# Key and value projections between the state products, the linear unit's result kept in SBUF, and the output stage's rows in the state operands' place

## The chip, the core and the metric

The kernel runs on one core of one Trainium2 chip. The metric is the device time of one execution in microseconds (us). The core has a matrix engine (TensorE, PE in the profile, with its weight loads shown apart as PEld), a vector engine (VectorE, DVE), an engine for activations (ScalarE, ACT), a general one (GpSimd, POOL) and a fifth that only issues transfers (SyncE, SP). Each engine works through its own instructions in order; semaphores tie them together. Transfers (DMAs) are issued here from SP and, for a few, from POOL. Tiles live in SBUF, results of matmuls in PSUM.

## The reference

One layer of an encoder over 1024 tokens of width 1024. After an input LayerNorm, one projection `h @ w_in` makes the operands of three mixers: retention (256 columns), a bidirectional linear state-space mixer, S5 (256), and windowed attention (512; 8 query heads, 2 key/value heads, a window of 128 tokens to each side). The mixers' results are concatenated, go through `w_out`, and a residual LayerNorm follows; a router then lets each of 16 experts take 128 tokens, the experts are SwiGLU networks (1024 to 2048 to 1024), and a last LayerNorm follows. What the change touches:

```python
# end of the S5 mixer
y = jax.nn.gelu(y + d * uf)                       # y: sum over both scan directions
gate = jax.nn.sigmoid(y @ w_glu + b_glu)          # gated linear unit
y_ssm = y * gate
# attention
scores = jnp.einsum('bcqkgd,bcskd->bckgqs', qb, kb) - slopes * jnp.abs(rel)
p = jnp.exp(scores - m)
# output projection
mix = jnp.concatenate([y_ret, y_ssm, y_att], axis=-1) @ w_out
```

## The kernel before

All matmuls that need float32 accuracy on large operands are done as three matmuls of rounded parts: each operand is split into a high part (ACT copies it to the rounded type) and a low part (DVE subtracts), helper `split`, lines 70 and 71, and `mm3`, lines 79 to 81.

The program has four stages.

1. The **front** (`front`, from L944; 0 to about 303 us). Input norm, all projections, retention, the S5 scan and the S5 output. Its order is written out by hand: every step is put at a place, a number, and `Plan.run` emits all steps sorted by place. So each engine's queue holds the instructions in the order of places, and an instruction that waits holds up everything behind it on its engine.
2. The **attention and output loop** (from L2233; about 303 to 480 us): eight tiles of 128 tokens, two rounds for each. `attention_scores` and `attention_exp` run two rounds ahead; `attention_out` normalizes, transposes and multiplies with the values; `out_proj_load` fetches a tile's operands; `out_proj_part` projects. This loop is not ordered by hand: a planner with its own costs orders it.
3. The last tile and the choice of tokens (`last_tile`), ordered by hand.
4. The experts (about 520 us to the end): 384 weight blocks of 1 MB, each loaded, split and multiplied.

The end of the front is what the change rewrites. Its steps there, in the order list of L1162 (letters as in the code): `q31` is the last query projection, `V0` and `V1` are the value projections of the two halves of the tokens, `K0` and `K1` the key projections (24 matmuls of 128x512 each), and `o0` to `o3` the four state products (`Output.product`, 16 pairs of weight load and matmul each, with the Gelu in `Output.put`, L819). The order before is `q31 V0 o0 K0 o1 V1 o2 K1 o3`.

- A state product needs a tile `MU` (m_d and u_d), a tile `W` (wo_d) and a tile `Z` (s_d), loaded from DRAM by SP. The operands of o0 and o1 (`MU`, `W`) and the `Z` of o0 lie in pool `s5m`. The rest lies in pool `s5o`, opened by `output_space` at place O, which comes after R; R is where `keys_space` closes the retention pools `retB` and `ret`, 15 places after r7, the last retention chunk. `s5o` gets memory that `retB` leaves, so its first writers wait for the last users of `retB`, among them the store of the last retention chunk (`Chunk.store`, L436, tile `roT`).
- `key_rows` (L857) splits the keys into partitions 0 to 63 of `KHL` and copies them to partitions 64 to 127, the high part on ACT (L864), the low part on DVE (L865).
- After o3 come the gated linear unit and the first two rounds of attention scores. `Output.turn` transposes the Gelu's result (L827) and ACT copies it (L828). `Output.gate` multiplies with `w_glu` in full float32 (L833). `Output.gated` does a Tanh on ACT (L841), a scale and shift on DVE (L842) and a product on DVE (L843), into `YO`. `YO` is stored to DRAM (L847), and `out_proj_load` reads it back tile by tile (L1376), together with the retention rows (L1374), and splits both in one pair of instructions of 512 columns.
- The splits of `w_out` (`Matrix.parts`, tile `WO`) lie among these steps; so do the two rounds of `attention_exp` (L1334 and L1336), both after all the gates.

Of the kernel before, what the change touches and what calls it, by code (L numbers as in the profile page):

```python
# [20 lines left out]
P = 128  # L21
# [326 lines left out]
class Chunk:  # L348
# [84 lines left out]
    def store(self):  # L433
        oT = self.K.retB.tile([P, 2, P], F32, name="roT", bufs=2)
        self.K.nc.scalar.activation(oT, self.pt[:, 0:2, :], AF.Copy)
        self.K.nc.sync.dma_start(self.K.y_dram[self.t], oT)  # L436
# [333 lines left out]
class Output:  # L770


    def __init__(self, K, I):
        self.K, self.I, self.x = K, I, {}

    def space(self, pool):
        K, I, self.pool = self.K, self.I, pool
        self.YG = pool.tile([P, 8, 256], F32, name="YG", tag="yg")
        self.wg = pool.tile([P, 2, 256], F32, name="wg")
        K.nc.sync.dma_start(self.wg, I["ssm_w_glu"])  # L780
        self.bg = pool.tile([P, 2], F32, name="bg")
        K.nc.sync.dma_start(self.bg, I["ssm_b_glu"])

    def bias(self):
        self.hb = self.pool.tile([P, 2], F32, name="hb")
        self.K.nc.vector.tensor_scalar(self.hb, self.bg, 0.5, None, op0=OP.mult)

    def load(self, g2, q, pool, bufs):
# [6 lines left out]
        w = pool.tile([P, 2, 4, 144], F32, name="W", bufs=bufs)  # L795
# [26 lines left out]
    def turn(self, m, q):  # L822
        if m == 0 and q == 0:
            self.yT = self.pool.tile([P, 2, 8, P], F32, name="yT")
# [3 lines left out]
        self.K.nc.scalar.activation(self.yT[:, m, q * 4:q * 4 + 4, :], pt, AF.Copy)  # L828

    def gate(self, m, q):  # L830
        self.pg = self.K.pmm.tile([P, 4, P], F32, name="mm")
        for c in range(2):
            self.K.nc.tensor.matmul(self.pg, self.wg[:, c, m * P:(m + 1) * P], self.yT[:, c, q * 4:q * 4 + 4, :],  # L833
                                    start=(c == 0), stop=(c == 1))

    def gated(self, m, q):
        K, nc = self.K, self.K.nc
        if m == 0 and q == 0:
            self.YO = self.pool.tile([P, 2, P, 8], F32, name="YO", tag="yg")
        g = self.pool.tile([P, 4, P], F32, name="glu", bufs=2)  # L840
        nc.scalar.activation(g, self.pg, AF.Tanh, bias=self.hb[:, m:m + 1], scale=0.5)  # L841
        nc.vector.tensor_scalar(g, g, 0.5, 0.5, op0=OP.mult, op1=OP.add)  # L842
        nc.vector.tensor_tensor(self.YO[:, m].rearrange("p k i -> p i k")[:, q * 4:q * 4 + 4, :], g,  # L843
                                self.yT[:, m, q * 4:q * 4 + 4, :], OP.mult)
# [12 lines left out]
def key_rows(K, p, half):  # L857
# [28 lines left out]
def attention_query(K, parts, u, half):  # L886
# [3 lines left out]
                                     op1=OP.subtract)  # L890
    qs = qs.rearrange("p s (a b) -> p s a b", a=4)
# [7 lines left out]
class Matrix:  # L899
# [10 lines left out]
    def parts(self, c):  # L910
# [4 lines left out]
        for i in range(2):  # L915
            hi, lo = (K.WO[s][c // 4][:, c % 4 + i, :] for s in range(2))
            split(K, hi, lo, self.raw[c][:, i, :])
# [26 lines left out]
def front(K, I, pool, close):  # L944
# [180 lines left out]
    qs = [(g2, q) for g2 in range(2) for q in range(2)]  # L1125
# [17 lines left out]
    at(e2 + 7.0, lambda: out.states(*qs[0], X["s5m"][1]))  # L1143
# [18 lines left out]
    order = "q00 g0 g1 q01 r0 q10 r1 g2 r2 g3 q11 r3 q20 g4 r4 g5 q21 r5 g6 r6 q30 g7 r7 q31 V0 o0 K0 o1 V1 o2 K1 o3".split()  # L1162
# [3 lines left out]
    for w in order:  # L1166
        where[w] = s
        if w[0] in "KVq":
# [20 lines left out]
        elif w[0] == "r":  # L1189
# [1168 lines left out]
```

## Time and profile before

| what | value |
|---|---|
| median of 3 runs | 1634.75 us (1632.62 to 1634.87) |
| the profiled execution, its own time | 1636.51 us |
| its span, first to last instruction | 1634.6 us |
| mean granted TensorE clock | 0.987 |
| PE busy | 1568.8 us (96%) |
| DVE busy | 1418.9 us (87%) |
| ACT busy | 1130.8 us (69%) |

| stretch of the span | PE busy | granted clock |
|---|---|---|
| 0 to 231 us (front up to r7) | 216.63 of 231 us | 0.99 |
| 231 to 303 us (end of the front) | 57.31 of 72 us | 0.92 |
| 303 to 480 us (loop) | 166.90 of 177 us | 0.98 |
| 480 to 520 us (last tile) | 34.67 of 40 us | 1.00 |
| 520 to 1634 us (experts) | 1093.29 of 1114 us | 0.99 |

The timeline lists instructions by their start in us from the start of the span, then their duration, engine, line, operation and tiles; square brackets give the idle time of the engine before it and what ended that. A row of the view by stretches gives the length, then the busy time of PE, PEld, DVE, ACT and POOL with the number of instructions, the granted clock of TensorE, the busy share of the DMA engines and GB/s.

### The profile page before, as it was taken

The numbers are of one execution on the slowest core, as the hardware profiler recorded it, in microseconds if no ns is written. First come the engines' busy times: TensorE is split into PE (matmuls) and PEld (weight loads), VectorE is DVE, ScalarE is ACT, GpSimd is POOL, SyncE is SP. The second block draws the span as 40 slices with busy tenths as digits, with TensorE's granted clock in tenths as the row PEclk, the third lists the DMA queues.
The fourth block names the chain that finished last, engine by engine and source line by source line (L and its number), as shares of the span: only waits on it lengthen the run. The fifth ranks groups of instructions, "written<-read, shape, count | busy, mean of one in ns | idle before, by whom it ended". The sixth has DMA issues, their size and how long they took to land.

```text
span 1634.6 us, 21145 instructions
## 1 busy us (share of the span) xinstructions
PE 1568.8 (96%) x7704; PEld 1290.4 (79%) x7704; DVE 1418.9 (87%) x1742; ACT 1130.8 (69%) x1276; POOL 210.1 (13%) x247
## 2 busy tenths in 40 slices
PE   6999998799998999999999999999999999999997
PEld 5887887587776788888888888888878788888885
DVE  7986863777789999898998989889989999999996
ACT  4645454875755677777777777777778788787873
POOL 4002110011011010101101011001213022120211
PEclk9999999899999999999999999999999999999998
DMA  5565476424227899999999999999999999999993
GB/s 179 202 162 138 117 226 195 141 78 149 65 91 293 313 369 386 399 401 386 378 384 381 384 377 377 379 412 411 405 403 404 405 410 414 417 414 408 410 412 151
DMA packets 103258, 507.83 MB, mean 311 GB/s; under 512 B 13041, under 2 KB 28145, under 8 KB 52466
## 3 DMA queue, kind: packets, MB, share of 16 engines
q1 hardware_dynamic: 87426, 476.60, 75.0%
q0 software_dynamic: 15728, 29.89, 6.3%
q8 instruction: 60, 0.98, 0.2%
q14 instruction: 44, 0.36, 0.1%
HBM read 462.40 MB, written 44.04 MB: 310 GB/s over the span
## 4 chain that ended last, share of the span: by engine, by line
PE 49%; DVE 22%; DMA 14%; issue 8%; ACT 5%; POOL 1%; SPq 0%; POOLq 0%; DVEq 0%; ACTq 0%
PE gu L1822 19%; DVE whl L1869 11%; PE y L1822 9%; DMA wraw<-in_exp_w_down 8%; PE mm L79 4%; PE mm L81 4%; PE mm L80 4%; DMA wraw<-in_exp_w_up 4%; ACT whl L1862 2%; DMA wraw<-in_exp_w_gate 2%; DVE hT L71 1%; PE po L1362 1%; PE tp L1807 1%; DVE hid L1904 1%; DVE pT L71 1%
## 5 line engine op out<-in xcount | busy, mean ns | idle before, releaser
L1869 DVE TENSOR_TENSOR whl<-wraw,whl 128x2048 fp32r<-128x2048 f32 x384 | 870.9, 2286 | 70.2 <-ACT whl L1862 68.1
L1862 ACT ACTIVATE whl<-wraw 128x2048 fp32r<-128x2048 f32 x384 | 735.8, 1919 | 248.3 <-PE gu L1822 62.4
L1822 PE MATMUL gu<-whl,xT 128*128 128x512 f32 x3072 | 732.2, 395 | 0.0
L1822 PEld LDWEIGHTS gu<-whl,xT 128*128 128x128 f32 x3072 | 571.0, 189 | 117.4
L1822 PE MATMUL y<-whl,hT 128*128 128x512 f32 x1536 | 359.1, 389 | 0.7 <-ACT hT L70 0.7
L1822 PEld LDWEIGHTS y<-whl,hT 128*128 128x128 f32 x1536 | 288.1, 188 | 60.7 <-ACT hT L70 0.9
L1786 POOL DMA_INDIRECT xs<-h_d,index x15 | 30.0, 1999 | 461.0 <-PE y L1822 301.4
L79 PE MATMUL mm<-hT,whl 128*128 128x512 f32 x160 | 65.7, 411 | 0.0
L70 ACT ACTIVATE hT<-tp 128x512 fp32r<-128x512 f32 x80 | 46.0, 583 | 26.8 <-PE tp L1807 13.7
L81 PE MATMUL mm<-hT,whl 128*128 128x512 f32 x160 | 62.5, 391 | 0.0
L80 PE MATMUL mm<-hT,whl 128*128 128x512 f32 x160 | 62.5, 391 | 0.0
L71 DVE TENSOR_TENSOR hT<-tp,hT 128x512 fp32r<-128x512 f32 x80 | 54.0, 682 | 5.4 <-ACT hT L70 5.3
L79 PE MATMUL mm<-WO,yh 128*128 128x512 f32 x128 | 51.6, 403 | 3.6 <-ACT yh L70 3.6
L80 PE MATMUL mm<-WO,yh 128*128 128x512 f32 x128 | 50.3, 393 | 0.0
L81 PE MATMUL mm<-WO,yl 128*128 128x512 f32 x128 | 48.9, 392 | 0.0
L1807 PE MATMUL tp<-ident,hid 128*128 128x128 f32 x256 | 39.3, 276 | 9.8 <-DVE hid L1904 9.7
L1807 PEld LDWEIGHTS tp<-ident,hid 128*128 128x128 f32 x256 | 31.3, 141 | 20.1 <-DVE hid L1904 13.1
L79 PE MATMUL mm<-whl,hT 128*128 128x512 f32 (+1 forms) x128 | 46.6, 364 | 0.1
L1336 ACT ACTIVATE S<-S,asm 128x384 f32<-128x384 f32 (+1 forms) x64 | 36.9, 579 | 13.0 <-DVE asm L1323 7.7
L81 PE MATMUL mm<-whl,hT 128*128 128x512 f32 (+1 forms) x128 | 44.0, 344 | 1.4 <-DVE hT L71 1.4
L1904 DVE TENSOR_TENSOR hid<-hid,gu 128x512 f32<-128x512 f32 x64 | 43.5, 680 | 1.5 <-PE gu L1822 1.4
L80 PE MATMUL mm<-whl,hT 128*128 128x512 f32 (+1 forms) x128 | 43.9, 343 | 0.8 <-DVE whl L135 0.8
(428 smaller groups left out, 1799.3 us busy)
## 6 DMA issues: line engine op xcount, KB each, us to landing
wraw<-in_exp_w_gate SPq DMA_DIRECT2D x128, 1024.0 KB, 8.1
wraw<-in_exp_w_up SPq DMA_DIRECT2D x128, 1024.0 KB, 8.5
wraw<-in_exp_w_down SPq DMA_DIRECT2D x128, 1024.0 KB, 8.8
wraw<-in_w_in SPq DMA_DIRECT2D x8, 1024.0 KB, 7.5
x<-in_x SPq DMA_DIRECT2D x8, 512.0 KB, 4.6
h_d<-x SPq DMA_DIRECT2D x8, 512.0 KB, 3.2
q_d<-kst SPq DMA_DIRECT2D x32, 128.0 KB, 2.7
wraw<-in_w_out SPq DMA_DIRECT2D x4, 1024.0 KB, 6.8
```

What stands on the lines that cost most here:

```text
L70: nc.scalar.activation(hi, src, AF.Copy)
L71: eng.tensor_tensor(lo, src, hi.bitcast(F32), OP.subtract)
L79: nc.tensor.matmul(ps, a[0], b[0], start=start, stop=False)
L80: nc.tensor.matmul(ps, a[0], b[1], start=False, stop=False)
L81: nc.tensor.matmul(ps, a[1], b[0], start=False, stop=stop)
L1336: nc.scalar.activation(S[g][:, :W], S[g][:, :W], AF.Exp, bias=nm[:, g:g + 1], accum_out=rs[:, g:g + 1])
L1786: K.nc.gpsimd.indirect_dma_start(out=xs, out_offset=None, in_=K.h1_dram, in_offset=bass.IndirectOffsetOnAxis(ap=K.index[:, e:e + 1], axis=0))
L1807: K.nc.tensor.transpose(pt[:, c, :], src[:, (c0 + c) * P:(c0 + c + 1) * P], K.ident)
L1822: nc.tensor.matmul(ps, a[s][c], u[:, t, i * w:(i + 1) * w], start=first and id(ps) not in began, stop=last and left[id(ps)] == 0)
L1862: self.K.nc.scalar.activation(u[:, 0, :], self.raw[k1].rearrange("p a b -> p (a b)"), AF.Copy)
L1869: self.K.nc.vector.tensor_tensor(u[:, 1, :], raw, u[:, 0, :].bitcast(F32), OP.subtract)
L1904: at(self.after, q, 3, lambda: nc.vector.tensor_tensor(self.h[q], self.h[q], self.pg[q][1], OP.mult))
```

## The change

- The order becomes `q31 V0 o0 K0 V1 K1`, and the other three state products follow K1 in a section with places of its own (A): o1, o2, o3 with the scores of round 0 and the transposes between them. The products are numbered anew, so that the first two give the columns of the first transposes.
- The last retention chunk is finished earlier (`norm`, `gated`, `turn`, `store` 2.2 to 4.5 places after its product; before 4 to 12), inside q31. Its store uses a tile of another pool. R moves to just before V0, so `s5o` opens there, on the other side of the memory, and all its loads are issued from there on, `MU` and `W` now as one tile `MUW`. The store of q31's query rows goes behind them.
- The second copy of the keys is made by a DMA that POOL issues, in place of L864 and L865.
- The linear unit: the transposed values are scaled by 0.5 as they are copied, half of these copies on DVE. The Tanh takes its input unscaled, and one DVE instruction, `(tanh + 1) * y`, takes the place of two. `YO` gets a pool of its own and stays in SBUF; its two stores and the loop's sixteen loads of it are gone; the loop splits retention rows and `YO` in two pairs of 256 columns.
- `w_out` is split block by block; the first four blocks during V1, the rest in section A. The scores and exponentials of rounds 0 and 1 are issued in halves, the exponentials between the Tanhs.
- A pool `opy` opens in the place of `s5m` after o3: it holds the retention rows of two tiles, loaded in advance, and `yh` and `yl`. The loads of ln1's gain and shift come after the loop's first `out_proj_load`.

```diff
@@ Chunk.store
-        oT = self.K.retB.tile([P, 2, P], F32, name="roT", bufs=2)
+        if self.t == NT - 1:
+            oT = self.K.ast.tile([P, 2, P], F32, name="roT", tag="q2", bufs=3)
+        else:
+            oT = self.K.retB.tile([P, 2, P], F32, name="roT", bufs=2)
@@ Output
+    def weights(self):
+        K, I = self.K, self.I
         K.nc.sync.dma_start(self.wg, I["ssm_w_glu"])
         K.nc.sync.dma_start(self.bg, I["ssm_b_glu"])
...
-        x = pool.tile([P, 8, P], F32, name="MU", bufs=bufs)
+        xw = pool.tile([P, 2176], F32, name="MUW", tag="muw", bufs=bufs)
+        x = xw[:, 0:1024].rearrange("p (a b) -> p a b", a=8)
...
-        self.K.nc.scalar.activation(self.yT[:, m, q * 4:q * 4 + 4, :], pt, AF.Copy)
+        dst = self.yT[:, m, q * 4:q * 4 + 4, :]
+        if eng:
+            self.K.nc.vector.tensor_scalar(dst, pt, 0.5, None, op0=OP.mult)
+        else:
+            self.K.nc.scalar.activation(dst, pt, AF.Copy, scale=0.5)
...
-        g = self.pool.tile([P, 4, P], F32, name="glu", bufs=2)
-        nc.scalar.activation(g, self.pg, AF.Tanh, bias=self.hb[:, m:m + 1], scale=0.5)
-        nc.vector.tensor_scalar(g, g, 0.5, 0.5, op0=OP.mult, op1=OP.add)
-        nc.vector.tensor_tensor(self.YO[:, m].rearrange("p k i -> p i k")[:, q * 4:q * 4 + 4, :], g,
-                                self.yT[:, m, q * 4:q * 4 + 4, :], OP.mult)
-
-    def store(self, m):
-        self.K.nc.sync.dma_start(self.K.y2_dram[m], self.YO[:, m].rearrange("p k i -> p (k i)"))
+        g = K.ast.tile([P, 4, P], F32, name="glu", tag="k4", bufs=3)
+        nc.scalar.activation(g, self.pg.pop((m, q)), AF.Tanh, bias=self.hb[:, m:m + 1], scale=1.0)
+        nc.vector.scalar_tensor_tensor(K.YO[:, m].rearrange("p k i -> p i k")[:, q * 4:q * 4 + 4, :], g, 1.0,
+                                       self.yT[:, m, q * 4:q * 4 + 4, :], op0=OP.add, op1=OP.mult)
@@ key_rows
-        nc.scalar.activation(K.KHL[kv][b, 0, hs], K.KHL[kv][a, 0, hs].bitcast(F32), AF.Copy)
-        nc.vector.tensor_copy(K.KHL[kv][b, 1, hs], K.KHL[kv][a, 1, hs].bitcast(F32))
+        nc.gpsimd.dma_start(K.KHL[kv][b, :, hs], K.KHL[kv][a, :, hs])
@@ front
-    qs = [(g2, q) for g2 in range(2) for q in range(2)]
+    qs = [(g2, q) for q in range(2) for g2 in range(2)]
...
-    order = "q00 ... q31 V0 o0 K0 o1 V1 o2 K1 o3".split()
+    order = "q00 g0 g1 q01 r0 q10 r1 g2 r2 g3 q11 r3 q20 g4 r4 g5 q21 r5 g6 r6 q30 g7 r7 q31 V0 o0 K0 V1 K1".split()
...
-            at(s + 4, c.norm)
-            at(s + 6, c.gated)
-            at(s + 9, c.turn)
-            at(s + (12 if c.t == NT - 1 else 14), c.store)
+            for gap, fn in zip((2.2, 3.0, 3.78, 4.5) if c.t == NT - 1 else (4, 6, 9, 14),
+                               (c.norm, c.gated, c.turn, c.store)):
+                at(s + gap, fn)
...
-    R = where["r7"] + 2.9 + 12.1
+    R = where["V0"] - 0.1
...
+    at(O + 0.01, lambda: out.states(*qs[1], X["s5o"][1], 2))
+    at(O + 0.02, lambda: out.load(*qs[2], X["s5o"][1], 1))
+    at(O + 0.03, out.weights)
+    at(where["o0"] + 3.1, lambda: (out.states(*qs[2], X["s5m"][1], 1), out.load(*qs[3], X["s5m"][1], 2)))
+    at(where["o0"] + 3.2, lambda: out.states(*qs[3], X["s5o"][1], 2))
+    at(where["K0"] + 1.0, out.bias)
...
+    for (g, e1), k in zip(((0.0, 2.75), (3.2, 5.0), (6.8, 9.55)), qs[1:]):
+        at(A + g, lambda k=k: out.product(*k))
+        at(A + e1, lambda k=k: out.put(*k))
+    for g, k in ((5.9, (0, 0)), (6.0, (0, 1)), (10.3, (1, 0)), (10.35, (1, 1))):
+        at(A + g, lambda k=k: out.turn(*k, k[1]))
+    for c, hi, lo in ((4, 2.8, 2.8), (5, 2.9, 2.9), (6, 6.9, 6.9), (7, 7.0, 12.9)):
+        at(A + hi, lambda c=c: mat.high(c))
+        at(A + lo + 0.01, lambda c=c: mat.low(c))
+    for g, i, g0 in ((2.7, 0, 0), (9.5, 0, 2), (11.4, 1, 0), (13.5, 1, 2)):
+        at(A + g, lambda i=i, g0=g0: attention_scores(K, i, g0, g0 + 2))
+    for g, e1, k in ((11.8, 13.6, (0, 0)), (14.0, 15.6, (1, 0)), (15.7, 17.3, (0, 1)), (17.4, 19.0, (1, 1))):
+        at(A + g, lambda k=k: out.gate(*k))
+        at(A + e1, lambda k=k: out.gated(*k))
+    for g, i, g0 in ((10.4, 0, 0), (13.7, 0, 2), (15.65, 1, 0), (17.35, 1, 2)):
+        at(A + g, lambda i=i, g0=g0: attention_exp(K, i, g0, g0 + 2))
+
+    def rows_space():
+        close(X["s5m"][0])
+        X["opy"] = pool("opy")
+        K.opy, K.y = X["opy"][1], {}
+        for t in range(2):
+            out_proj_rows(K, t)
+    at(A + 9.6, rows_space)
@@ out_proj_load
-    y = pool.tile([P, 4, P], F32, name="y")
-    nc.sync.dma_start(y[:, 0:2, :], K.y_dram[t])
-    for m in range(2):
-        nc.sync.dma_start(y[:, 2 + m, :], K.y2_dram[m][:, t * P:(t + 1) * P])
...
-    split(K, yh[:, 0:4, :], yl[:, 0:4, :], y)
+    split(K, yh[:, 0:2, :], yl[:, 0:2, :], y)
+    split(K, yh[:, 2:4, :], yl[:, 2:4, :], K.YO[:, :, t * 16:(t + 1) * 16, :].rearrange("p m k i -> p m (k i)"))
...
+    if t + 2 < NT:
+        out_proj_rows(K, t + 2)
```

More of the change, by code (lines that the diff above doesn't have):

```diff
@@ L914, in parts, with low, part @@
                 K.WO[s].append(K.hy.tile([P, KC // 2, D], F32R, name=f"WO{s}", tag="hy"))
-        for i in range(2):
-            hi, lo = (K.WO[s][c // 4][:, c % 4 + i, :] for s in range(2))
-            split(K, hi, lo, self.raw[c][:, i, :])
+        K.nc.scalar.activation(K.WO[0][c // 4][:, c % 4, :], self.raw[c - c % 2][:, c % 2, :], AF.Copy)
+    def low(self, c):
+        K = self.K
+        hi, lo = (K.WO[s][c // 4][:, c % 4, :] for s in range(2))
+        K.nc.vector.tensor_tensor(lo, self.raw[c - c % 2][:, c % 2, :], hi.bitcast(F32), OP.subtract)
+    def part(self, c):
+        self.high(c)
+        self.low(c)
 class Rows:
@@ L1228, in keys_space @@
         K.AV = X["kv"][1].tile([P, NT, 2, 2, 64], F32R, name="AV")
+        X["yo"] = pool("yo", side="right")
+        K.YO = X["yo"][1].tile([P, 2, P, 8], F32, name="YO")
     at(R, keys_space)
@@ L1234, in output_space @@
     def output_space():
-        X["s5o"] = pool("s5o")
+        X["s5o"] = pool("s5o", side="right")
         out.space(X["s5o"][1])
-        out.bias()
     at(O, output_space)
-    at(O + 0.01, lambda: out.load(*qs[2], X["s5o"][1], 1))
-    at(O + 0.02, lambda: out.states(*qs[1], X["s5o"][1]))
-    at(where["o0"] + 3.1, lambda: (out.states(*qs[2], X["s5m"][1]), out.load(*qs[3], X["s5m"][1], 2)))
-    at(where["o1"] + 3.1, lambda: out.states(*qs[3], X["s5o"][1]))
-    G = s + 0.3
-    mq = [(m, q) for q in range(2) for m in range(2)]
-    for q in range(2):
-        at(where["K1"] + 1.9 + q * 1.9 - 0.01, lambda q=q: out.turn(0, q))
-        at(G + q * 0.5, lambda q=q: out.turn(1, q))
-    for i, k in enumerate(mq):
-        at(G + 1.7 + i * 2.0, lambda k=k: out.gate(*k))
-        at(G + 3.7 + i * 2.0, lambda k=k: out.gated(*k))
-    at(G + 11.0, lambda: (out.store(0), out.store(1)))
-    at(G + 15.0, lambda: close(X["s5o"][0], X["s5m"][0]))
+    at(O + 0.01, lambda: out.states(*qs[1], X["s5o"][1], 2))
[4 more added lines that the diff above has]
+    at(where["K0"] + 1.0, out.bias)
     mat = Matrix(K, I)
@@ L1257, in front @@
     at(where["q31"] + 8.2, lambda: mat.load(2))
-    at(where["o1"] + 0.3, lambda: (mat.parts(0), mat.load(4)))
-    at(where["K1"] + 3.0, lambda: (mat.parts(2), mat.load(6)))
-    at(G + 1.2, lambda: mat.parts(4))
-    at(G + 5.0, lambda: mat.parts(6))
+    for i, c in enumerate((0, 1)):
+        at(where["V1"] + 1.7 + i, lambda c=c: mat.part(c))
+    at(where["V1"] + 2.8, lambda: mat.load(4))
+    for i, c in enumerate((2, 3)):
+        at(where["V1"] + 3.7 + i, lambda c=c: mat.part(c))
+    at(where["V1"] + 4.8, lambda: mat.load(6))
@@ L1307, in attention_scores @@
     W, ro, k0 = (b1 - b0) * P, (b0 - c + 1) * P, b0 * P
-    qs = K.Q.pop(i)
-    sm = K.small.tile([P, 5, 4], F32, name="asm", bufs=3)
+    if g0 == 0:
+        K.P[i] = [], K.small.tile([P, 5, 4], F32, name="asm", bufs=3)
+    S, sm = K.P[i]
+    qs = K.Q[i]
     m, nm, rs, es, rd = (sm[:, k] for k in range(5))
     hs = slice(kv * 4, kv * 4 + 4)
-    S = []
-    for g in range(4):
+    for g in range(g0, g1):
         h = kv * 4 + g
@@ L2176, in build @@
     K.y_dram = [dr.tile([P, 2, P], F32, name=f"y_d{t}") for t in range(NT)]
-    K.y2_dram = [dr.tile([P, L], F32, name=f"y2_d{m}") for m in range(2)]
     K.q_dram = [[dr.tile([P, 4, 4, P], F32, name=f"q_d{h}_{k}") for k in range(2)] for h in range(2)]
```

84 lines of the change are left out of this document (45 added, 39 removed).

## The prediction

> **What bounds the kernel now.** I read the granted clock first (0.987 in the mean), then the busy time by stretches, then PE's timeline where PE is least busy, then ACT, DVE and SP at the same place. PE is busy for 96% of the span, so what the change can win is PE's idle time at the end of the front, and whatever slows PE there.
>
> ```profile
> span 1634.6 us, 21145 instructions
> PE 1568.8 (96%) x7704; PEld 1290.4 (79%) x7704; DVE 1418.9 (87%) x1742; ACT 1130.8 (69%) x1276; POOL 210.1 (13%) x247
> ```
>
> By stretches (length, then busy time of PE, PEld, DVE, ACT, POOL, then clock, DMA share, GB/s):
>
> ```profile
> 253.02:302.83 49.81, 35.12 (x181) 28.09 (x180) 26.43 (x55) 26.10 (x50) 3.65 (x10) 0.88 0.51 163
> 259.15:263.87 4.72, 4.72 (x22) 4.72 (x23) 1.75 (x2) 0.31 (x1) 0.00 (x0) 0.50 1.06 407
> 269.51:272.19 2.68, 2.68 (x26) 2.68 (x24) 0.00 (x0) 0.60 (x1) 0.00 (x0) 1.00 0.00 0
> 302.83:310.60 7.77, 7.74 (x32) 6.50 (x33) 5.10 (x18) 7.77 (x22) 0.77 (x1) 0.64 0.98 349
> 320.00:480.00 160.00, 150.43 (x807) 123.81 (x805) 125.37 (x329) 103.57 (x253) 17.18 (x45) 0.99 0.29 92
> 400.00:420.00 20.00, 16.73 (x87) 13.65 (x86) 13.61 (x42) 11.05 (x27) 2.69 (x7) 0.91 0.41 120
> ```
>
> The first row runs from the start of o1 to the loop's first transposes. Of its 49.81 us PE idles 49.81 - 35.12 = 14.69. The second row is o1 after its wait, the third is o2, the same work: 2.68 us at clock 1.00. PE's timeline says where the idle time lies:
>
> ```profile
> 231.28 0.49 PE L79 MATMUL mm<-hT,whl 128*128 128x512 f32 x1
> 236.63 0.39 PE L81 MATMUL mm<-hT,whl 128*128 128x512 f32 x1
> 253.02 0.49 PE L812 MATMUL mm<-MU 128*128 128x128 f32 x2
> 259.15 1.23 PE L815 MATMUL mm<-W,Z 128*128 128x128 f32 x4 [5.64 <-DMA Z<-s_d]
> 283.26 0.39 PE L1316 MATMUL at<-KHL,qs 128*128 128x256 f32 x1 [0.90 <-DVE asm L1320]
> 284.01 1.03 PE L827 MATMUL tp<-ident,YG 128*128 128x128 f32 x8
> 285.87 0.39 PE L1316 MATMUL at<-KHL,qs 128*128 128x256 f32 x1 [0.35 <-DVE asm L1320]
> 286.61 3.60 PE L833 MATMUL mm<-yT,wg 128*128 128x512 f32 x8
> 289.64 0.74 PE L1316 MATMUL at<-KHL,qs 128*128 128x384 f32 x1
> 290.74 3.60 PE L833 MATMUL mm<-yT,wg 128*128 128x512 f32 x8
> 302.83 1.97 PE L1355 MATMUL tp<-ident,S 128*128 128x128 f32 x8 [7.80 <-ACT S L1349]
> ```
>
> Two waits carry it. Product o1 waits 5.64 us for its `Z`. The loop's first transposes wait 7.80 us for ACT, which at the end of the gated linear unit runs behind DVE, then loads a table, then does both rounds of exponentials in one row:
>
> ```profile
> 251.08 1.28 ACT L819 ACT_TABLE_LOAD   x1 [2.79 <-DMA y_d<-roT]
> 282.36 0.60 ACT L819 ACTIVATE YG<-mm 128x512 f32<-128x512 f32 x1
> 288.53 0.69 ACT L841 ACTIVATE glu<-mm,hb 128x512 f32<-128x512 f32 x1 [0.91 <-PE mm L833]
> 296.16 0.69 ACT L841 ACTIVATE glu<-mm,hb 128x512 f32<-128x512 f32 x1 [2.81 <-DVE YO L843]
> 296.86 1.28 ACT L1334 ACT_TABLE_LOAD   x1
> 298.15 0.20 ACT L1334 ACTIVATE asm<-asm 128x4 f32<-128x4 f32 x1
> 302.29 3.29 ACT L1349 ACTIVATE S<-S,asm 128x256 f32<-128x256 f32 x8
> ```
>
> The late `Z` goes back to SP: the store of the last retention chunk holds the memory of `s5o`. From the chain of waits, SP's timeline and the view of transfers (KB each, median us to landing):
>
> ```profile
> 239.34 1.15 SPq L436 DMA_DIRECT2D y_d<-roT  x2
> 241.66 2.53 SPq L895 DMA_DIRECT2D q_d<-kst  x4
> 245.47 5.52 DMA y_d<-roT
> 251.07 0.33 SPq L780 DMA_DIRECT2D wg<-in_ssm_w_glu  x1
> 253.82 1.86 SPq L804 DMA_DIRECT2D Z<-s_d  x4
> wraw<-in_w_out SPq DMA_DIRECT2D x4, 1024.0 KB, 6.8
> Z<-s_d SPq DMA_DIRECT2D x8, 256.0 KB, 5.1
> qs<-q_d POOLq DMA_DIRECT2D x8, 256.0 KB, 3.3
> ```
>
> **The change part by part.** All sums go against the profiled execution's own 1636.51 us, whose span is 1634.6; the median of the runs is 1634.75, or 1.76 less, and I carry the difference over.
>
> *The wait for `Z` goes.* In the new order SP issues, right behind the last retention store, two `Z`, four for `MUW`, `wg`, `bg`, the `w_out` block, four query stores, and then eight more for o2 and o3: 21 issues at 0.47 (1.86 / 4) to 0.63 us (2.53 / 4), some 10.6 us. The first may have to wait for the store of chunk 6, the second of the two at 239.34 (begun about 239.9, so landed by 245.4 at the 5.52 us of its successor). So the queue is through at about 256, and the last `Z` lands 5.1 us later, at 261. PE reaches o1 only after K0, V1 and K1. Counting from the present end of K0 (253.02) these are 48 matmuls at 0.23 us ((236.63 - 231.28) / 23) and one group of transposes, about 11.6 us: 264.6 at the earliest. So all of `Z`, `MUW` and `wg` is there: -5.64 us. Behind it, DVE's `bias` waits for `bg` (issued about 249, landed about 252) ahead of the split of K0, which isn't ready before 253: nothing.
>
> *The slow clock goes with it.* After the wait the row shows clock 0.50, and o1 took 4.72 + 0.49 us where o2 takes 2.68: -2.53 us. In the new order no wait that long is left.
>
> *The other three waits.* The two short ones (0.90, 0.35) are scores that wait for DVE with two PSUM tiles; in halves, with a product or a gate between, the two pieces have 0.9 us and more in between: -1.25. The long one takes a race of PE and ACT from the end of o3 on. PE then has the scores (three halves of about 0.75, by the spacing 283.26 to 284.01), two groups of transposes (half of 0.87 each, as the next instruction shows at 284.80), four gates (half of 289.64 - 286.61 = 1.51 each), and the four heads of round 2, which the planner puts there now already (289.64 to 290.74 and the like at 293.77: 2.2): 2.25 + 0.87 + 6.06 + 2.2 = 11.4 us. ACT has the last Gelu (0.60), transposes to wait for (0.45), a copy (0.60), the table (1.28), the eight exponentials with their sums (302.29 - 298.15 = 4.14), four Tanhs (about 0.6 each when back to back: 2.4) and the first normalization (0.4): 9.9 us, and some gaps. So PE is the later one, by a little: of 7.80 us I take all but 0.5. If the planner leaves round 2 behind, PE waits up to 1 us there and does that work later.
>
> *What comes in.* Chunk 7's transposes now lie ahead of the last third of q31. Its chain isn't shortened: the gated values end at 235.52 + 0.42, while PE gets there at 231.28 + 18 x 0.23 = 235.4: +0.6. `turn` after o3 waits for the Gelu (0.60) behind scores of 0.75: +0.1. The Tanh's scale on DVE (four of 0.43) and the copies of the keys (L864, L865) fall away beside PE's work: 0. The copies become DMAs from POOL, bounded by the query loads of equal size (issue 0.75, landing 3.3 us): K0's are ready near 260 and first read near 268; K1's serve only chunk 2 and later, tens of us on: 0 at either bound.
>
> ```profile
> 235.52 0.42 DVE L425 TENSOR_TENSOR ro<-ro,gate 128x256 f32<-128x256 f32 x1 [1.42 <-ACT ro L421]
> 294.52 0.43 DVE L842 TENSOR_SCALAR glu<-glu 128x512 f32<-128x512 f32 x1
> L435 ACT ACTIVATE roT<-tp x8: 378/386/399, 182.6 to 245.1; 128x256 f32<-128x256 f32 x8
> L71 DVE TENSOR_TENSOR yl<-y,yh 128x512 fp32r<-128x512 f32 x8 | 5.5, 684 | 0.1
> L70 ACT ACTIVATE yh<-y 128x512 fp32r<-128x512 f32 x8 | 5.0, 626 | 2.7 <-PE mm L80 2.0 <-ACT asm L1334 0.7
> ```
>
> *The loop.* After 302.83 PE ran at clock 0.64 for 7.77 us, at most 2.8 us lost; but ACT is busy for all of these 7.77 us, so a faster PE waits for ACT. Between 0 and -2.8 I take -0.4, near ACT's row. Two splits of 256 columns in place of one of 512 cost ACT 2 x 0.386 - 0.626 = 0.15 and DVE 2 x 0.42 - 0.684 = 0.16 us a tile, 2.4 us for eight at most; PE is busy 150.43 of 160 us there, so I take +0.4. The stores and 16 loads of `YO` that fall away ended nobody's wait on PE in this stretch: 0. Everything behind the loop, the first weight loads too, is issued relative to the loop's rounds and moves along whole.
>
> Sum: -5.64 - 2.53 - 1.25 - 7.3 + 0.7 - 0.4 + 0.4 = -16.0 us; 1636.5 - 16.0 = 1620.5 for the profiled execution, and 1618.7 by the median.
>
> **The rivals.**
>
> *A, the loop gives a part back.* The planner orders the loop anew from another starting point. For it: stretches differ now; 400 to 420 loses 3.27 us of PE, the other seven of the loop (160 - 150.43 - 3.27) / 7 = 0.9 each. Against it: the loop's work is nearly the same. Two more stretches like that cost 2 x 2.4: -11.3, 1623.4.
>
> *B, the loads aren't early.* If SP is held until 251 as now, the state operands still arrive in time (251 + 10.6 + 5.1 = 267 for the last, needed at 272), but the second `w_out` block is issued near 255.5 and lands 6.8 later, at 262.3. ACT's split of it stands ahead of V1's copy, whose transposes PE wants at 261.3; ACT needs about 2.6 us for split and copy: +3.6, 1622.3. For it: the row at 251.07; against it: chunk 7's store no longer uses that memory.
>
> *C, tables.* The new order runs exp, Tanh, exp, Tanh and so on. One load at 251.08 served Gelu and all Tanhs; exp needed the one at 296.86. If exp and Tanh share no table, there are eight loads in place of one before the first normalization's end and a ninth behind it: +8 x 1.28 = 10.2 us on ACT, of which 1.5 are absorbed by PE's longer path: +8.7, 1627.4. No row decides it. The Trainium skill, ScalarE: Activation LUTs, section "Table sets: the hidden batching unit", lists tanh in the set of exp, and by that the extra loads don't come; the same page ("What ACT_TABLE_LOAD costs") puts a switch at about 2.66 us with its drain, by which eight would cost 21 us and the kernel would be slower. The rows here show no such drain: the load at 296.86 begins as the Tanh ends (296.16 + 0.69) and the next ACTIVATE starts at 298.15.
>
> *D, slower.* The loop becomes bound by the chain ACT, DVE, PE throughout: the doubled splits and the shifted start make every stretch of it like 400 to 420. Then it loses 8 x 3.27 = 26.2 us where it loses 9.57 now, +16.6, and the doubled splits are on the path, +2.0 more than I took: -16.0 + 18.6 = +2.6, 1637.3. It decides from 2.0 us of added PE idle time in each 20 us of the loop on. For it: such a stretch exists. Against it: the other seven.
>
> **How the numbers follow.** The forecast, 76%, own range 1615.5 to 1622 (lower with the full 2.8 us of clock, upper with B's or the splits' upper bound); A 8%, B 4%, C 4%, D 5%, and 3% for a loop that the planner orders better, some 5 us beyond the forecast. 1611.5 to 1626.5 leaves out C, D and the tails. About 0.2% of the time, 3.3 us, is what a measurement can tell from no change. Faster: all but D and a part of A that goes near it, 0.93; the same 0.02; slower 0.05.
>
> **What would show it.** Right: o1 starts with no wait for `Z`, at clock 1.00, about 265; no idle time over 1.5 us on PE between 232 and 290; the loop's first transposes begin about 286 to 287; one table load between the last Gelu and the loop. SP issues `Z` for o1 before 247. Wrong in the first part: PE waits at V1's transposes (B) or ACT shows table loads between Tanhs (C). Wrong in the second: the first transposes come 16 us earlier, but the last tile does not, and PE's idle time between has grown (A, D).

## The result: 1618.3 us, and the profile after

| | before | after |
|---|---|---|
| median (runs, lowest to highest), us | 1633.76 (6, 1632.62 to 1635.86) | 1618.3 (6, 1611.29 to 1624.7) |
| profiled execution, its own time / span, us | 1636.51 / 1634.6 | 1621.39 / 1619.6 |
| first transposes of the loop, us | 302.83 | 290.69 |
| fifth tile's first router transposes in the loop, us | 441.84 | 426.78 |
| experts' first hidden transposes, us | 522.25 | 508.25 |

The ratio of the times is 0.9904, 95% interval 0.9877 to 0.9931: faster by about 1%, with 1618.7 forecast. The six runs after scatter over 13 us, the six before over 3. In the later series, of 11 to 17 runs, the kernel before scatters over 9 to 10 us too, so the scatter did not come with the change; it is the subject of the last experiments.

The head of the page of the kernel after, as quoted of before:

```profile
span 1619.6 us, 21109 instructions
PE 1563.2 (97%) x7704; PEld 1287.0 (79%) x7704; DVE 1416.6 (87%) x1744; ACT 1128.5 (70%) x1278; POOL 208.2 (13%) x251
```

PE's timeline of the kernel after, from the end of the projection to the experts (start, length, then what ended the idle time before):

```profile
235.52 0.41 PE L431 MATMUL tp<-ident,ro 128*128 128x128 f32 x2 [0.48 <-DVE ro L425]
...
264.44 0.38 PE L820 MATMUL mm<-MUW 128*128 128x128 f32 x2
...
266.67 0.61 PE L823 MATMUL mm<-MUW,Z 128*128 128x128 f32 x4
...
271.99 0.36 PE L1352 MATMUL at<-KHL,qs 128*128 128x256 f32 x1 [4.71 <-DMA qs<-q_d]
...
281.23 1.09 PE L835 MATMUL tp<-ident,YG 128*128 128x128 f32 x8 [0.22 <-ACT YG L827]
...
290.69 0.60 PE L1393 MATMUL tp<-ident,S 128*128 128x128 f32 x4
...
292.18 0.48 PE L79 MATMUL mm<-WO,yh 128*128 128x512 f32 x1
...
508.25 1.11 PE L1850 MATMUL tp<-ident,hid 128*128 128x128 f32 x4 [5.58 <-DVE hid L1947]
```

All four waits of before are gone: o1 begins at 264.44 and its products with `Z` follow without one, no score waits for DVE, and the loop's first transposes carry no bracket. In their place stands one new wait: the first scores wait 4.71 us for the queries. By stretches (columns as in the prediction):

```profile
253.26:290.69 37.43, 32.49 (x177) 26.27 (x176) 21.89 (x45) 22.27 (x43) 6.23 (x9) 0.95 0.85 203
264.44:267.36 2.92, 2.84 (x25) 2.64 (x23) 1.38 (x2) 1.23 (x3) 0.60 (x1) 1.00 1.10 372
272.35:276.82 4.47, 4.47 (x27) 4.47 (x27) 3.19 (x6) 0.00 (x0) 0.00 (x0) 0.63 0.90 99
277.70:280.30 2.60, 2.60 (x27) 2.60 (x25) 1.90 (x2) 2.30 (x3) 0.00 (x0) 1.00 0.01 3
```

The stretch from the end of K0 to the loop, 49.81 us before, takes 37.43, and PE's idle time in it fell from 14.69 to 4.94. The second row is o1, now at clock 1.00; the third is o2 behind the new wait, at 0.63 and 4.47 us; the fourth is o3, the same work at 1.00 in 2.60. So the slow clock moved with the wait: 1.87 us beside the 4.71.

Who is late is seen in the timeline of POOL and SP, and in one row of the chain of waits (start, length):

```profile
242.95 0.80 SPq L812 DMA_DIRECT2D Z<-s_d  x2
254.87 0.67 POOL L870 DMA_DIRECT2D KHL<-KHL  x1 [21.54 <-DVE KHL L71]
...
257.02 1.52 POOL L1314 DMA_DIRECT2D qs<-q_d  x2 [0.20 <-DMA MUW<-m_d]
```

```profile
257.02 14.84 DMA qs<-q_d
```

and in the transfers between 240 and 300 us (KB each, median us to landing):

```profile
KHL<-KHL POOLq DMA_DIRECT2D x4, 256.0 KB, 9.3
qs<-q_d POOLq DMA_DIRECT2D x6, 256.0 KB, 8.5
```

POOL waits until 254.87 for the split keys, issues the two copies into the other 64 partitions, and only then, at 257.02, the first two query loads. The first of them lands 14.84 us later, where the query loads of before had 3.3 by the median. The two copies had landed by then, at 262.8 and 265.7.

ACT at the end of the linear unit:

```profile
282.54 1.28 ACT L1372 ACT_TABLE_LOAD   x1
284.93 0.71 ACT L70 ACTIVATE yh<-y 128x256 fp32r<-128x256 f32 x2
285.54 0.67 ACT L851 ACTIVATE glu<-mm,hb 128x512 f32<-128x512 f32 x1
286.11 0.50 ACT L1374 ACTIVATE S<-S,asm 128x256 f32<-128x256 f32 x1
```

Behind one load a Tanh (L851) and an exponential (L1374) follow each other with no further load: rival C's condition does not hold, and this row agrees with what the Trainium skill, ScalarE: Activation LUTs, section "Table sets: the hidden batching unit", says of tanh in the set of exp. `yh` of the first tile is split already here, since the retention rows came early and the unit's half lies in SBUF.

The loop up to the fifth tile's first router transposes, before and after, with its first 20 us after:

```profile
302.83:441.84 139.01, 132.14 (x689) 109.11 (x689) 107.81 (x300) 97.56 (x246) 15.44 (x35) 0.97 0.37 114
```

```profile
290.69:426.78 136.09, 128.60 (x694) 106.30 (x692) 109.10 (x308) 98.92 (x254) 16.47 (x42) 1.00 0.36 107
290.69:310.69 20.00, 18.16 (x95) 14.60 (x94) 16.54 (x46) 18.01 (x47) 2.96 (x9) 1.00 0.60 172
```

So the 14.0 us that the front and the loop won (522.25 to 508.25) are 12.14 up to the loop's first transposes and 2.92 in these rows, less 1.06 from there to the experts (80.41 before, 81.47 after, from the table). In these rows PE is busy 3.54 us less at clock 1.00 in place of 0.97, and idle 0.62 us more. Up to the last tile's first router transposes, at 487.55 and 472.56, it is 184.72 us before and 181.87 after: 2.85 less, so the rest of the loop adds nothing. The span fell by 15.0, the median by 15.5.

### The profile page after: what moved, and what is told of

The parts are those of the page before. It is cut to its first block, busy times and chain, and to the rows that moved or that the text cites. A ratio compares the mean times of both kernels' runs of the same rounds, so it can differ in the third digit from the quotient of the medians.

```text
span 1619.6 us, 21109 instructions
## 1 busy us (share of the span) xinstructions
PE 1563.2 (97%) x7704; PEld 1287.0 (79%) x7704; DVE 1416.6 (87%) x1744; ACT 1128.5 (70%) x1278; POOL 208.2 (13%) x251
## 4 chain that ended last, share of the span: by engine, by line
PE 54%; DVE 19%; DMA 13%; issue 7%; ACT 5%; POOL 1%; SPq 0%; POOLq 0%; DVEq 0%; ACTq 0%
PE gu L1865 24%; PE y L1865 12%; DVE whl L1912 9%; DMA wraw<-in_exp_w_down 7%; PE mm L81 4%; PE mm L79 4%; PE mm L80 3%; ACT whl L1905 2%; DMA wraw<-in_exp_w_gate 2%; DMA wraw<-in_exp_w_up 2%; PE tp L1850 1%; DVE hT L71 1%; ACT S L1374 1%; DMA qs<-q_d 1%; PE po L1400 1%
## 5 line engine op out<-in xcount | busy, mean ns | idle before, releaser
L1356 DVE CUSTOM_DVE_ANT_0 S<-at,R,sink 128x384 f32<-128x384 f32 (+1 forms) x64 | 35.6, 579 | 10.3 <-PE at L1353 9.2
```

What stands on the lines that cost most here:

```text
L1356: nc.vector.tensor_tensor_reduce(s[:, :W], ps[:, :W], K.R[:, ro:ro + W], 2.0 ** -(h + 1), K.sink[:, h:h + 1], OP.add, OP.max, accum_out=m[ ...
```

## The experiments

All edits stand against the kernel after, unless said otherwise. "The front's end" is the start of the experts' first hidden transposes, 508.25 above. It is the finer measure: in three profiles of the same kernel after it lay at 508.25, 507.60 and 509.34.

### Where the new wait comes from

First the kernel after once more, as the measure for the others.

> The changed kernel again, on the chip of the next three, to size the scatter of its runs (1611 to 1625 us in six). Theory Q: the scatter comes from the wait of the scores of round 0 for their query rows, 4.71 us in the profile, which lie behind the key copies in POOL's transfer queue; then the profiled wait of this execution differs from 4.71 by some us, and its span by as much. Rival W: the scatter comes from the experts' weight loads; then the wait is again 4 to 5 us whatever the span.

1616.98 us (6 runs, 1610.45 to 1619.48); ratio 0.9885, interval 0.9864 to 0.9907. The wait for the queries is there again, 4.11 us.

**The queries issued ahead of the key copies.**

```
-    for i in range(3):
-        at(where["K1"] + 3.0 + i * 0.1, lambda i=i: attention_queries(K, i))
+    for i, place in enumerate((where["K0"] + 2.0, where["K0"] + 2.1, A + 9.7)):
+        at(place, lambda i=i: attention_queries(K, i))
```

> The query loads of rounds 0 and 1 are issued by POOL early in K0, ahead of K0's key copies; that of round 2 follows the scores of round 0. Theory Q: the wait of 4.71 us on PE is gone, and with it the slow clock behind it (o2 took 4.05 us where o3 took 2.60), so 5 to 6 us less than the changed kernel, about 1612.5 us, and a narrower scatter. Rival W: PE's wait goes but the scatter stays at 10 us or more. Rival A (ACT bounds the part behind o3): the gain at the first transposes is under 2 us.

The loop's first transposes, and its transfers between 240 and 300 us:

```profile
285.30 0.60 PE L1393 MATMUL tp<-ident,S 128*128 128x128 f32 x4
```

```profile
qs<-q_d POOLq DMA_DIRECT2D x6, 256.0 KB, 4.2
KHL<-KHL POOLq DMA_DIRECT2D x4, 256.0 KB, 7.0
```

The wait is gone. The first transposes come at 285.30, 5.4 us earlier than in the kernel after, and the front ends at 501.75, 5.9 to 7.6 us before its three profiles. The time is 1616.94 us (6 runs, 1611.59 to 1619.91; ratio 0.989, 0.9869 to 0.9912): nothing of it is seen there.

**The key copies by ACT and DVE again**, as before the change.

```
-        nc.gpsimd.dma_start(K.KHL[kv][b, :, hs], K.KHL[kv][a, :, hs])
+        nc.scalar.activation(K.KHL[kv][b, 0, hs], K.KHL[kv][a, 0, hs].bitcast(F32), AF.Copy)
+        nc.vector.tensor_copy(K.KHL[kv][b, 1, hs], K.KHL[kv][a, 1, hs].bitcast(F32))
```

> The second copy of the keys is made by ACT and DVE again, as before the change; all else is the changed kernel. Theory Q: nothing is ahead of the query loads, which land in 3 to 6 us, PE's wait goes, and the copies (1.15 us on ACT and 0.76 us on DVE for each half) are hidden behind V1 and cost at most 1.9 us behind K1, where the Gelu of o1 waits for them: 4 to 6 us less than the changed kernel. Rival L (the transfer engines are simply overloaded by SP's loads between 250 and 270 us): the query loads still take over 10 us to land and a wait of 3 us or more stays.

```profile
260.89 0.66 PE L883 MATMUL tp<-ident,va 128*128 128x128 f32 x4 [0.28 <-ACT va L876]
```

In this PE timeline there is no wait for queries either; the copies on the engines cost 0.28 us at V1's transposes and nothing else. The first transposes come at 284.52, the front ends at 500.96; 1617.56 us (6 runs, 1612.54 to 1621.77), ratio 0.9894, 0.9873 to 0.9915.

**The same copies, issued by SP** in place of POOL (the DMA stays, the queue is another).

```
-        nc.gpsimd.dma_start(K.KHL[kv][b, :, hs], K.KHL[kv][a, :, hs])
+        nc.sync.dma_start(K.KHL[kv][b, :, hs].bitcast(F32), K.KHL[kv][a, :, hs].bitcast(F32))
```

> The changed kernel with the key copies issued by SP instead of POOL; they move the same bytes at the same time, but the query loads no longer queue behind them. Read at the experts' first transposes of hidden rows (507.6 and 508.25 us in two profiles of the changed kernel, 501.75 with the queries first). Theory Q (order in POOL's queue): PE's wait for the query rows falls below 1 us and that point comes at 502 to 503. Rival L (the transfer engines are overloaded): the query loads still land 10 us or more after their issue and the point stays at 506 or later.

Its transfers between 240 and 300 us:

```profile
qs<-q_d POOLq DMA_DIRECT2D x7, 256.0 KB, 4.7
KHL<-KHL SPq DMA_DIRECT2D x4, 256.0 KB, 8.6
```

The copies are as slow as before (8.6 us), and yet the wait for the queries is gone: the first transposes come at 285.75, the front ends at 502.82 (one time, 1619.61 us). So it is not the copies that the scores wait for, but the place of the query loads behind them among POOL's instructions. Two things go together in that place, the later issue and the slow landing. With the copies issued by SP, POOL issues the first two query loads at 243.9 and 248.8, and they land 8.3 and 9.3 us later, long before the scores; in the kernel after it comes to them at 257.02. With the 3.3 us of before, loads issued at 257.02 and done issuing at 258.54 would have been there by 262, ahead of the scores at 267.3; so the late issue costs because the landing is slow there too.

Whether it is slow because copies lie ahead in POOL's queue can be read from other query loads. Three of them, from the views of transfers: issued at 262.20 with the copies issued by SP, at 262.06 with the copies on the engines, and at 275.57 in the kernel with the late close (below), there right behind two key copies in POOL's queue.

```profile
qs<-q_d POOLq DMA_DIRECT2D x1, 256.0 KB, 14.7
qs<-q_d POOLq DMA_DIRECT2D x1, 256.0 KB, 6.4
qs<-q_d POOLq DMA_DIRECT2D x1, 256.0 KB, 4.2
```

The first has no copy ahead of it in its queue and is the slowest; in the kernel after, the load issued at 261.66 took 13.1. The third comes right behind copies and is the fastest; with the queries first, a load right behind copies, issued at 268.70, took 7.2. So copies ahead in the queue are neither needed for a slow landing nor enough for one. What the slow cases have in common is what else is under way: copies, from whichever queue, together with two blocks of `w_out`. The copies' own landing varies in the same way. The last two with the late close, issued at 273.63 and 274.98 behind the blocks of `w_out`, landed in 2.9 and 4.2 us; the four in the kernel after took 7.9 to 9.7. Which part of the DMA engines or of SBUF sets these times isn't shown.

### Whether the other terms are real

**Both rounds of exponentials behind the last Tanh**, in one row as before the change; the rest stays.

```
-    for g, i, g0 in ((10.4, 0, 0), (13.7, 0, 2), (15.65, 1, 0), (17.35, 1, 2)):
-        at(A + g, lambda i=i, g0=g0: attention_exp(K, i, g0, g0 + 2))
+    for i in range(2):
+        at(A + 19.1 + i * 0.1, lambda i=i: attention_exp(K, i))
```

> The exponentials of rounds 0 and 1 follow the last Tanh in one row, as before the change, instead of lying between the Tanhs. Theory of the prediction (the wait of 7.80 us came from ACT's row of table load and exponentials behind the last Tanh): PE waits 4 to 7 us for ACT ahead of the first transposes, and runs slower behind this: 5 to 8 us more than the changed kernel. Rival (ACT has the same work in either order and bounds the start of the loop): within 2 us of the changed kernel.

Its timeline of PE, with ACT's table load:

```profile
289.03 1.28 ACT L1372 ACT_TABLE_LOAD   x1
294.91 0.50 PE L79 MATMUL mm<-WO,yh 128*128 128x512 f32 x1 [3.15 <-ACT yh L70]
297.81 1.03 PE L1393 MATMUL tp<-ident,S 128*128 128x128 f32 x8
```

The table is loaded behind the last Tanh again. PE does projection work in the meantime, waits 3.15 us for ACT's split `yh`, and the first transposes come 7.1 us later (297.81 to 290.69), although the wait for the queries happened to be 2.56 in this profile and not 4.71. The front ends at 513.65, 4.3 to 6.1 us later than in the three profiles of the kernel after. This is the term of the long wait: it is the interleaving of exponentials and gates that wins it. The time, 1629.93 us (12 runs, 1619.77 to 1633.99; ratio 0.9972, 0.9954 to 0.999), rose by 13 against the kernel after, more than the front explains.

**The late close of the state operands' memory**, on top of the queries first: the last chunk's store from the old place, its steps and the loads at the old times.

```
-        if self.t == NT - 1:
-            oT = self.K.ast.tile([P, 2, P], F32, name="roT", tag="q2", bufs=3)
-        else:
-            oT = self.K.retB.tile([P, 2, P], F32, name="roT", bufs=2)
+        oT = self.K.retB.tile([P, 2, P], F32, name="roT", bufs=2)
...
-            for gap, fn in zip((2.2, 3.0, 3.78, 4.5) if c.t == NT - 1 else (4, 6, 9, 14),
+            for gap, fn in zip((4, 6, 9, 12) if c.t == NT - 1 else (4, 6, 9, 14),
...
-    R = where["V0"] - 0.1
+    R = where["r7"] + 2.9 + 12.1
```

> The kernel with the queries first, and in it the early end of the last retention chunk is undone: its steps, its store and the place R are those of before, so the state operands are loaded from about 251 us on; the order of the products stays new. The prediction's rival B: V1's transposes wait 3 to 4 us for the second w_out block's split on ACT, and the experts' first transposes come at about 505.4 instead of 501.75. The other way: the new order alone hides the loads, within 1 us of 501.75.

Its timeline of ACT, DVE and PE:

```profile
253.24 1.28 ACT L824 ACT_TABLE_LOAD   x1 [4.93 <-DMA y_d<-roT]
255.18 0.50 PE L79 MATMUL mm<-hT,whl 128*128 128x512 f32 x1 [2.02 <-ACT YG L824]
262.05 0.17 DVE L790 TENSOR_SCALAR hb<-bg 128x2 f32<-128x2 f32 x1 [13.02 <-DMA Z<-s_d]
262.84 0.59 ACT L70 ACTIVATE KHL<-mm 64x512 fp32r<-64x512 f32 x1 [7.23 <-DVE KHL L71]
264.30 0.47 PE L79 MATMUL mm<-hT,whl 128*128 128x512 f32 x1 [1.74 <-DVE KHL L71]
267.90 0.66 PE L879 MATMUL tp<-ident,va 128*128 128x128 f32 x4 [1.30 <-ACT va L872]
```

The front ends at 507.82, 6.1 us behind the queries first alone (501.75); one time of 1624.58 us. So the early close is worth some 6 us, but by three waits of 2.02, 1.74 and 1.30 us and what follows them, and `Z` isn't among them: the first Gelu writes into the memory that the late store still holds (the 4.93 us at ACT's table load), and then DVE stands idle for 13.02 us at the gate's bias (L790), which comes ahead of the key split in its order and needs a late load, `bg`, issued at 256.46 and landed 5.5 us later (the bracket names the `Z` that landed at about the same time); the split follows at 262.13.

**The linear unit through DRAM again**: `YO` is stored at the end of the unit, and each tile's rows (both halves) are loaded one tile ahead into one buffer and split at once. The rows loaded early fall away with it.

```
-        for t in range(2):
-            out_proj_rows(K, t)
     at(A + 9.6, rows_space)
+    def unit_store():
+        for m in range(2):
+            nc.sync.dma_start(K.y2_dram[m], K.YO[:, m].rearrange("p k i -> p (k i)"))
+        out_proj_rows(K, 0)
+    at(A + 19.2, unit_store)
...
-    K.y[t] = K.opy.tile([P, 2, P], F32, name="y", bufs=2)
-    K.nc.sync.dma_start(K.y[t], K.y_dram[t])
+    K.y[t] = K.opy.tile([P, 4, P], F32, name="y", bufs=1)
+    K.nc.sync.dma_start(K.y[t][:, 0:2, :], K.y_dram[t])
+    for m in range(2):
+        K.nc.sync.dma_start(K.y[t][:, 2 + m, :], K.y2_dram[m][:, t * P:(t + 1) * P])
...
-    split(K, yh[:, 0:2, :], yl[:, 0:2, :], y)
-    split(K, yh[:, 2:4, :], yl[:, 2:4, :], K.YO[:, :, t * 16:(t + 1) * 16, :].rearrange("p m k i -> p m (k i)"))
+    split(K, yh[:, 0:4, :], yl[:, 0:4, :], y)
```

> The changed kernel with the linear unit's result stored to DRAM after the last Tanh and read back tile by tile in the loop, with the retention rows, one split of 512 columns instead of two of 256, one tile ahead. The prediction's term (0 for the stores and loads, +0.4 for the doubled splits): the experts' first transposes within 1 us of the changed kernel's 507.6 to 508.25. Rival: the first tile's rows come some 8 us later than now (store 1.7 and 2.6, load 0.9 and 2.9 us) and PE has nothing else, so 3 us or more later.

Its PE timeline, and stretches of 10 us (in the kernel after, PE is busy for 18.16 of the first 20 us at clock 1.00, so idle for 1.84):

```profile
305.19 0.80 PE L79 MATMUL mm<-WO,yh 128*128 128x512 f32 x1
```

```profile
291.00:301.00 10.00, 8.35 (x41) 5.32 (x39) 9.38 (x30) 9.31 (x27) 2.36 (x9) 1.00 0.81 235
301.00:311.00 10.00, 8.40 (x33) 6.46 (x34) 5.29 (x11) 8.42 (x19) 0.59 (x1) 0.83 0.88 265
```

The first transposes come at 290.96, as in the kernel after; but the projection starts at 305.19 in place of 292.18, and PE is idle for 1.65 and 1.60 us of these two stretches, the second of them at clock 0.83. The loop up to the fifth tile takes 140.6 us (290.96 to 431.52) in place of 136.09, and the front ends at 511.69, 2.4 to 4.1 us later than in the kernel after (one time, 1624.89 us). Keeping the unit and loading the rows early is worth 4.5 us in the loop by this, and 2.4 to 4.1 at the front's end. Of the 4.5 us, 1.8 are more idle time of PE (9.3 in place of 7.5), of which 1.4 at the loop's start; the rest is that PE is busy longer with the same work (131.25 in place of 128.60). At the loop's start the projection is what PE can do while it would wait for ACT. The stores, the early rows and the split into two were not tried apart.

### Why a front that ends 6 us earlier isn't seen in the time

The three kernels again, on one chip:

> The changed kernel beside the next two on one chip, to see whether a front that is 6 us shorter makes the kernel 6 us shorter. Its front's end (the experts' first transposes of hidden rows) at 507.6 to 508.3; 1617 to 1618 us.

> Queries first, again. Theory S (what follows the front moves along whole, and the scatter of the weight loads hides it in a few runs): over both series 4 to 7 us less than the changed kernel. Rival T (the experts' stretch gives the time back): again within 2 us of the changed kernel, the experts' stretch 5 us longer.

> Key copies on ACT and DVE, again; its front ends 6.6 us earlier than the changed kernel's. Theory S: over both series 4 to 7 us less than the changed kernel. Rival T: again within 2 us of it.

| | front's end, us | median, us (runs; lowest to highest) | ratio, 95% interval |
|---|---|---|---|
| after | 509.34 | 1616.81 (5; 1614.51 to 1619.99) | 0.9899, 0.9879 to 0.9919 |
| queries first | 502.49 | 1617.16 (5; 1613.83 to 1618.79) | 0.9902, 0.9884 to 0.992 |
| copies on the engines | 503.46 | 1615.75 (6; 1609.12 to 1624.59) | 0.9883, 0.986 to 0.9906 |

Again the front ends earlier, by 6.9 and 5.9 us, and again the times can't be told apart. Scatter alone doesn't hide that much: over both series the mean of 11 runs with the queries first is 1616.5 and of 12 with the copies on the engines 1616.7, against 1617.2 for 17 runs of the kernel after. The runs of each deviate by some 3 to 4 us from their mean, so the means are known to about 1 us, and 6 us would show. Something behind the front takes it back, in the mean. From first to last, the 64 hidden products on DVE (groups by line, with the first and the last start, of the kernel after and of the copies on the engines in the second series):

```profile
L1947 DVE TENSOR_TENSOR hid<-hid,gu x64: 669/680/689, 507.5 to 1599.1; 128x512 f32<-128x512 f32 x64
```

```profile
L1948 DVE TENSOR_TENSOR hid<-hid,gu x64: 669/681/689, 502.7 to 1604.2; 128x512 f32<-128x512 f32 x64
```

They take 1091.6 and 1101.5 us: one stretch of the same work, in which nothing was edited, differs by 10 us. The kernel after itself took 1091.6, 1089.7 and 1088.7 in its three profiles, the copies on the engines 1096.4 and 1101.5, the queries first 1091.0 and 1091.2. So with the copies on the engines both profiles lose there about what the front had won (4.8 us or more); with the queries first neither does, and their two profiled executions were indeed fast (1613.16 and 1613.83 us, against 1621.39, 1617.15 and 1617.88 for the kernel after), while the mean of their nine other runs, 1617.1, is no lower than that of the fourteen others of the kernel after, 1616.9. The profiles differ late: in all 12 profiles whose experts are unedited, the first 32 products take 555.6 to 559.6 us, the last 32 from 532.2 to 542.8. In this second half (experts 9 to 16) the DMA engines are busy throughout (the row of the kernel after in the second series; DMA share and GB/s stand last; from 520 to 1060 us the share is 0.98, with 382 GB/s):

```profile
1060.00:1590.00 530.00, 529.19 (x2416) 436.75 (x2415) 499.64 (x303) 420.91 (x322) 94.93 (x74) 1.00 1.00 409
```

Beside the weights run the loads, stores and gathers of the final normalization. So I took that of the eight tiles away, under both orders of the queries; the rows of the output that no late expert writes are left out.

```
-            for t in range(NT):
-                final_norm(self, t, q + 4 * t + 2)
```

> The changed kernel without the final normalization of the eight tiles beside the last experts: the rows of the output that no late expert writes are left out, with their loads, stores and work of ACT and DVE. Theory F (the scatter and the give-back of the earlier front lie in these transfers and steps): the runs agree within some 3 us in place of 10, the time falls by up to some 10 us, and the next kernel (the same with the queries first) is 4 to 6 us faster than this one. Theory W (they lie in the experts' weight loads, which stay): the scatter stays near 10 us and the next kernel takes the same time within 2 us.

> The kernel with the queries first, and without the final normalization of the eight tiles (left out as in the run before). Its front ends near 502 us, 6 us before the changed kernel's. Theory F: 4 to 6 us faster than the run before, with little scatter. Theory W: the same time as the run before within 2 us, scatter near 10 us.

1616.01 us (6 runs, 1607.76 to 1616.94; ratio 0.9878, 0.9853 to 0.9903) and, queries first, 1612.21 us (5 runs, 1609.78 to 1613.76; ratio 0.9864, 0.9842 to 0.9887). What ACT waits for between 1060 and 1595 us (us in total, times, longest), in the kernel after (second series) and in the first of these:

```profile
ACT whl L1905 <- DMA wraw<-in_exp_w_down: 31.4, 38, 1.8
ACT whl L1905 <- PE gu L1865: 23.5, 40, 0.8
ACT whl L1905 <- DMA wraw<-in_exp_w_up: 18.8, 20, 1.6
ACT whl L1905 <- DMA wraw<-in_exp_w_gate: 15.9, 13, 2.8
```

```profile
ACT whl L1905 <- PE gu L1865: 59.1, 87, 0.8
...
ACT whl L1905 <- DMA wraw<-in_exp_w_down: 21.5, 18, 2.0
ACT whl L1905 <- DMA wraw<-in_exp_w_up: 5.0, 5, 1.7
ACT whl L1905 <- DMA wraw<-in_exp_w_gate: 3.2, 5, 1.1
```

With the final normalization ACT waits 66.1 us for weights, without it 29.7, and then mostly for PE. The 64 hidden products take 1082.5 and 1082.9 us without it. So in the last eight experts the weight loads, slowed by those transfers, often come last, and that is where a run can lose some us. But the question itself isn't settled: the two fronts lie 5.8 us apart (508.28 and 502.45), the two medians 3.8, and the intervals of the two ratios overlap; that is between the theories. Nor did the scatter clearly go (9.2 and 4.0 us between lowest and highest). What stays open is why, with the normalization, the mean of 11 runs with the queries first (1616.5) is only 0.7 us below that of 17 runs of the kernel after (1617.2). No version here beats the kernel after by more than the scatter.

## Why the prediction was right, point by point

- **The wait for `Z` goes (-5.64), and the slow clock with it (-2.53).** Held. SP issues `Z` for o1 at 242.95 (forecast: before 247), PE comes to o1 at 264.44 (264.6), and o1 takes 2.92 us at clock 1.00.
- **The two short waits (-1.25).** Held: no score waits for DVE.
- **The long wait (-7.3 of 7.80).** Held: PE comes to the first transposes without idle time. The kernel with the exponentials last shows that it is a race: with them behind the last Tanh, the transposes come 7.1 us later.
- **What comes in (+0.7).** Chunk 7's transposes wait 0.48 (forecast 0.6), `turn` after o3 0.22 (0.1).
- **Copies and query loads by POOL ("0 at either bound").** This step failed. I bounded the copies by a load of equal size, and took the scores to depend on the copies alone. The copies landed in 7.9 and 9.5 us, not 3.3, and still came in time, at 262.8 and 265.7, ahead of the scores at 267.3. The query loads did not: I had not followed them past the copies among POOL's instructions. They were issued at 257.02, behind POOL's wait of 21.54 us for the split keys, and the first landed 14.84 us later: a wait of 4.71, and 1.87 us of slow clock after it. The landing of 3.3 us was also taken from a quieter stretch; the loads of the late close show that a copy or a query load is as fast as that when less is under way. Taking the wait away moves the first transposes to 285.30, 284.52 or 285.75 by three different edits, where the forecast had 286 to 287; with it they came at 290.69. That was the mark "no idle time over 1.5 us on PE between 232 and 290", and it was missed.
- **The loop (-0.4 + 0.4 = 0).** The term was mis-sized: -2.92. Of "between 0 and -2.8" for the slow clock I took -0.4, since ACT was busy for all of that time, so that a faster PE would wait for it. PE does not wait: it does projection work from 292.18 on, on rows that are already there. The kernel with the unit through DRAM takes these rows away and loses 4.5 us in the loop; that `YO`'s stores and loads "ended nobody's wait" was true of before, and no bound for the new start. The doubled splits are not seen as a loss.
- **Everything behind the loop moves along whole.** From before to after nearly so: the front's end came 14.0 us earlier, the median 15.5. For the three edits that brought the front's end 6 us further forward the time didn't follow. This step was argued, and it doesn't hold in general; why is open.

So the total, 0.4 us from the forecast, is right partly because errors cancel: a new wait worth some 6 us that I didn't see, against 17.5 us (302.83 to 285.30) in place of 16.0 up to the loop without it, and 2.9 in the loop in place of 0. That they cancel so closely is luck.

Of the rivals, A and D are refuted by the loop's rows (136.09 us in place of 139.01 up to the fifth tile, 181.87 in place of 184.72 up to the last) and C by ACT's. B's condition did not come, as `Z` was issued early; the kernel with the late close shows that the early close matters more than B had it, 6.1 us at the front's end in place of 3.6, and by other waits: the Gelu's memory and the order on DVE come ahead of V1's copy.

## What to carry to other kernels

When a load is moved, follow it in the queue that issues it: a DMA that must wait for an engine's result, ahead of it in the same queue, delays it as a busy engine would (POOL waited 21.54 us here). Its landing time of before no longer holds either, if it is issued into a busier stretch: price a load or a copy by what else is under way when it runs, not by its size alone. A fixed point ahead of a noisy stage shows what an edit does up to there, but not that the total follows. And when a wait on an engine is taken away at the start of a stage, ask what ready work the bound engine has there: rows loaded early gave PE work where it would have waited for ACT, and kept its clock at 1.00.

## What the runs showed of the hardware that I had not expected

- Copies of 256 KB from 64 partitions of SBUF to the other 64 landed in 9.3 us (median of 4 in the kernel after), 8.6 when issued by SP, 7.0 with the queries ahead. With the late close, where the last two ran behind the blocks of `w_out`, these took 2.9 and 4.2 us. Query loads of 256 KB into all partitions took 3.3 us in the kernel before.
- Query loads issued while such copies and two blocks of `w_out` were under way took 13.1 to 15.8 us in the kernel after, and 14.7 with no copy ahead of them in their queue; one issued right behind two copies took 4.2 us with the late close. With the blocks but without the copies one took 6.4.
- The first 32 hidden products of the experts, with a DMA share of 0.98 (382 GB/s), took 555.6 to 559.6 us in 12 profiles; the last 32, with 1.00 (409 GB/s), 532.2 to 542.8, though no instruction of them was edited.
